# Even tokens first in each block, and mixer B's far keys kept by parity, in one softmax

## The chip, the cores and the metric

One of the eight cores of a Trainium2 chip runs the whole kernel. Its engines are TensorE (PE, with its weight loads, PEld), VectorE (DVE), ScalarE (ACT), GpSimd (POOL) and SyncE (SP); each works through its own instructions in order and waits for the others through semaphores. All DMAs here are issued by SP. The metric is the device time of one execution in microseconds (us); two kernels are compared by runs on the same chip.

## The reference

One decoder block on 1024 tokens with a model width of 1024, in float32:

- modulated RMS norm of x, and one projection to the queries, keys and values of two mixers
- mixer A: 8 query heads on 2 key/value heads, each query sees the last 128 keys, with a sink in the denominator
- mixer B: 8 heads of width 64, a mixture of three dilated windows:

```python
B_BRANCHES = ((128, 1), (512, 4), (2048, 16))
for window, d in B_BRANCHES:
    # query t attends keys t, t-d, ..., t-(window//d)*d
    o, lse = banded_attention(to_sub(q), to_sub(k), to_sub(v), window // d, return_lse=True)
w = softmax(stack(lses))            # branches weighted by their softmax denominators
ob = sum(w * stack(outs))
```

- RMS norm of both mixers' outputs, an output projection, a norm, a gate and the residual; then an MLP (1024 to 4096, squared ReLU, back) with norms, a gate and the residual.

Weighting the branches by their denominators is the same as one softmax over all causal keys in which a key counts as often as branches reach it: 0 to 3 times. A key more than 128 back is reached only by d = 4 and d = 16, so its distance is a multiple of 4.

## The kernel before, in words

The kernel is one program for one core. A planner (`Sched`) runs while the program is built: each step has an engine, a planned duration, events it depends on, buffers it takes (`Res`) and gives back, and a priority. The planner plays the clocks of the engines forward and emits each engine's instructions in the order that this gives. On the chip that order is fixed. PE has several streams (`dense`, `s`, `t`, `pv` and others), among which `prefer` chooses: projections go first while attention is less than 0.8 units behind them, attention otherwise.

The projection is cut into six units u: 0 and 1 are mixer A's, 2 to 5 mixer B's, two heads each. Attention on a unit runs while the next units are projected. Float32 precision comes from operands split into a high and a low part, each product being two or three matmuls.

Attention of mixer B goes by items (u, tp, h): one head h and one pair tp (0 to 3) of query blocks of 128 tokens. Most items come in the order of u and tp; the item (4, 3, 1) comes after (5, 0, 1). Each item takes these steps:

- `s_b`: for each of the two query blocks qb, the scores of all (qb+1) x 128 keys, in chunks of up to 512 columns of one PSUM bank (L1240, PE; two banks, `r_s`). On each chunk one DVE instruction adds a mask with the logarithm of how often a key counts, writes the row to `p_sb` and takes the running minimum of the negated scores into `mn` (L1259). ACT takes the exponential and its sum (L1266), DVE the reciprocal (L1269), POOL scales the row (L1271).
- `t_pv`: in tp+1 chunks, each of two key blocks, PE transposes the probabilities of both query blocks (L1345, L1348), ACT copies the high part and DVE makes the low part (`ph`, L1359 and L1363), and PE multiplies with v (L1375, L1378, L1380). The stationary operand holds v's high and low parts side by side, so the output has 128 rows; the moving operand is the high and then the low part of the probabilities, 256 columns each.
- at the end of an item ACT copies the 64 rows of v's low part out of PSUM (L1407), DVE adds the 64 others (L1411), and SP stores the head's output to DRAM (L1414).

A probability buffer (`p_sb`, NP = 4 of them) holds an item's two rows for tp below 2, one row otherwise. In `evac` the projected v is transposed to tokens by rows and split (`vs`, L936 and L939). After the last projection eight output blocks (`out_block`, L1606 to L1717) begin as soon as their heads are done, and then the MLP runs in products of half matrices (L2093 to L2095 and the sums around them). `finish` stores the result, 128 tokens by 512 columns at a time (L2211).

Of the kernel before, what the change touches and what calls it, by code (L numbers as in the profile page):

```python
# [10 lines left out]
F32 = mybir.dt.float32  # L11
# [47 lines left out]
CW_MA = CW_MB + 1024  # L59
# [36 lines left out]
def _host(inputs):  # L96
# [14 lines left out]
    h["positions"] = np.ascontiguousarray(inputs["positions"][0].reshape(TB, P).T)  # L111
# [5 lines left out]
def _constants(c):  # L117
    c[:, CW_ID:CW_ID + P] = np.eye(P, dtype=np.float32)
    p = np.arange(P)[:, None]
    d = p + 896 - np.arange(1024)[None, :]  # L120
    mult = ((d >= 0) & (d <= 128)).astype(int)
    mult += (d >= 0) & (d <= 512) & (d % 4 == 0)
    mult += (d >= 0) & (d % 16 == 0)
    neg = np.array([BIG, 0.0, -np.log(2.0), -np.log(3.0)], np.float32)
    c[:, CW_MB:CW_MB + 1024] = neg[mult]
    d = p + P - np.arange(256)[None, :]
    c[:, CW_MA:CW_MA + 256] = np.where((d >= 0) & (d <= 127), 0.0, BIG)
# [267 lines left out]
def hybrid_block(ctx: ExitStack, tc: tile.TileContext, x, positions, w_ada, b_ada, g_attn_post, w_in, w_out,  # L395
# [33 lines left out]
    WR, WS, NP, NV, NK, NQ, NT, NO = 6, 2, 4, 3, 2, 2, 2, 2  # L429
# [3 lines left out]
    r_vt = Res(1)  # L433
    r_v, r_k, r_q, r_p, r_ph, r_ot, r_tmp = Res(NV), Res(0), Res(0), Res(NP), Res(NT), Res(NO), Res(1)
# [38 lines left out]
    vring = pool("vring", NV, "right", stack=rightv)  # L473
    prp = pool("prp", 1, stack=left1)
# [352 lines left out]
    qs, ks, vs, e_q, e_k, n_in = {}, {}, {}, {}, {}, {}  # L827

    acc_at = [(pj, "pj", r_pj)] * 2 + [(po, "o", r_o)] + [(psp, "s", r_s)] * 2 + [(pt, "t", r_t)]

    def evac(u, x, c, get_ps, done, r_bank):
# [109 lines left out]
        op("DVE", t_dv(256 * nh), f_vl, [e], gives=[(r_x, 1)], prio=2, after=posted)  # L941
# [110 lines left out]
    def open_attention():  # L1052
# [14 lines left out]
        masks = mkp.tile([P, 1280], F32, name="masks")  # L1067
        e_mask = load(lambda: nc.sync.dma_start(masks[:], consts[:, CW_MB:CW_MB + 1280]), 655360, prio=-20)
        mask_b = masks[:, 0:1024]
        mask_a = masks[:, 1024:1280]  # L1070
# [124 lines left out]
    UB = 2 * (2 * (0.108 + 0.117 + 0.173 + 4 * 0.227 + 0.108 + 0.117 + 0.173 + 0.227) + 0.107 * 36 + 0.43 * 10)  # L1195
# [5 lines left out]
    def count(it):  # L1201
        return it[1] + 1 if it[0] > 1 else (2 if it[1] else 1)
# [13 lines left out]
    def s_b(i, it, rec):  # L1216
        u, tp, h = it
        shared = tp < 2
        rec.e_p = []
        rec.held = 1 if shared else 2  # L1220
        for qi in range(2):
            qb = 2 * tp + qi
            W = (qb + 1) * P
            last_mn = None
            b = {}
            for c0 in range(0, W, 512):
                m = c0 // 512
                cw = min(512, W - c0)
                end = c0 + cw == W

                def f_s(c0=c0, cw=cw, m=m, qi=qi, qb=qb, W=W, b=b):
                    if m == 0:
                        if qi == 0 or not shared:
                            rec.tile = pprob.tile([P, 4 * 257], F32, name="p_sb", tag="p")
                        off = 2 * tp * P + P if shared and qi else 0
                        rec.p.append(rec.tile[:, off:off + W])
                        b["mn"] = small.tile([P, 2], F32, name="mn", tag="mn")
                    s = b["s", m] = psp.tile([P, 512], F32, name="s_ps", tag="s")
                    for hl in range(2):
                        T.matmul(s[:, :cw], qs[u, qb // 4][:, 2 * h + hl, qb % 4 * P:qb % 4 * P + P],  # L1240
                                 ks[u][:, h, c0:c0 + cw], start=(hl == 0), stop=(hl == 1))
                d = 2 * t_mm(cw)
                deps = e_k[u, c0 // 512] + e_q[u, qb // 4]
# [11 lines left out]
                e = pe_op("s", d, f_s, deps, takes=[(r_s, 1), (r_p, slot)], gives=gives, after=after)  # L1255

                def f_max(c0=c0, cw=cw, m=m, qi=qi, W=W, b=b):
                    mn = b["mn"]
                    V.tensor_tensor_reduce(rec.p[qi][:, c0:c0 + cw], b["s", m][:, :cw],  # L1259
                                           mask_b[:, 1024 - W + c0:1024 - W + c0 + cw], 1.0,  # L1260
# [1020 lines left out]
```

## Time and profile before

| what | us |
|---|---|
| runs of the kernel before | 1117.45, 1117.54, 1118.25 |
| median | 1117.54 |
| span of the profiled execution, first to last instruction | 1114.9 |
| median less span | 2.6 |
| PE busy | 1100.5 |
| DVE busy | 818.7 |
| ACT busy | 630.2 |

The span is that of the one execution that was profiled; its time from outside isn't listed apart from the three runs, and the 2.6 us stand for what lies around the span. Times in the profile count from the first instruction. Projections run from about 20 to 372 us, mixer B's scores from 161 to 406, output blocks from 372 to 493, the MLP from 493 to 1106.

### The profile page before, as it was taken

How to read it: one execution, taken by the hardware profiler on the slowest of the kernel's cores; microseconds unless marked ns; L12 is line 12 of the kernel's file. 1: busy time of each engine (PE TensorE's matmuls, PEld its weight loads, DVE VectorE, ACT ScalarE, POOL GpSimd, SP SyncE). 2: the span in 40 equal slices, each digit the busy share in tenths (PEclk: the TensorE clock that was granted, in tenths of full speed). 3: DMA queues.
4: the chain of work that ended last, by engine and by line, in shares of the span. 5: the costliest groups of instructions: out<-in, count | busy, mean ns of one | idle time of the engine just before them, and what ended most of it. 6: DMA issues, size and time to landing. Idle time of an engine off the chain costs nothing.

```text
span 1114.9 us, 15568 instructions
## 1 busy us (share of the span) xinstructions
PE 1100.5 (99%) x5393; PEld 917.4 (82%) x5393; DVE 818.7 (73%) x1386; ACT 630.2 (57%) x1092; POOL 249.7 (22%) x318
## 2 busy tenths in 40 slices
PE   8999999999999999999999999999999999999996
PEld 7788888888888888888888888888888888888885
DVE  7877776666777666689798654798643996537998
ACT  8768776464656666577674335643154632347542
POOL 2158768666742231110000000000000000000003
PEclk9999999999999999999999999999999999999998
DMA  9766667464513734656751369521578013584104
GB/s 350 216 193 189 196 218 233 154 207 157 189 41 143 259 108 129 226 214 241 279 216 38 108 241 330 180 76 40 199 269 308 26 57 113 189 319 153 39 19 151
DMA packets 94110, 195.39 MB, mean 175 GB/s; under 512 B 9008, under 2 KB 31664, under 8 KB 94032
## 3 DMA queue, kind: packets, MB, share of 16 engines
q1 hardware_dynamic: 94032, 194.40, 50.4%
q8 instruction: 43, 0.70, 0.3%
q14 instruction: 35, 0.29, 0.1%
HBM read 141.80 MB, written 33.03 MB: 157 GB/s over the span
## 4 chain that ended last, share of the span: by engine, by line
PE 86%; DVE 8%; issue 2%; ACT 1%; DMA 1%; POOL 0%; SPq 0%; POOLq 0%; DVEq 0%; ACTq 0%
PE mlp_ps L2094 17%; PE mlp_ps L2095 17%; PE mlp_ps L2093 17%; PE pj L957 5%; PE pj L960 5%; PE pj L958 4%; PE s_ps L1240 3%; PE y_ps L1647 2%; PE y_ps L1649 2%; PE y_ps L1648 2%; PE o_ps L1375 2%; PE pt_ps L1345 1%; PE s_ps L1295 1%; PE o_ps L1387 1%; PE pt_ps L1352 1%
## 5 line engine op out<-in xcount | busy, mean ns | idle before, releaser
L2093 PE MATMUL mlp_ps<-hw 128*128 128x512 f32 x896 | 348.9, 389 | 0.1
L2094 PE MATMUL mlp_ps<-hw 128*128 128x512 f32 x896 | 348.6, 389 | 0.0
L2095 PE MATMUL mlp_ps<-hw 128*128 128x512 f32 x896 | 348.6, 389 | 0.0
L2093 PEld LDWEIGHTS mlp_ps<-hw 128*128 128x128 f32 x896 | 168.2, 188 | 35.8 <-DVE u L2130 0.6
L2094 PEld LDWEIGHTS mlp_ps<-hw 128*128 128x128 f32 x896 | 168.2, 188 | 35.0
L2095 PEld LDWEIGHTS mlp_ps<-hw 128*128 128x128 f32 x896 | 168.2, 188 | 34.6
L1857 DVE TENSOR_TENSOR hw<-w,hw 128x1024 fp32r<-128x1024 f32 x96 | 114.7, 1222 | 96.5 <-ACT hw L1850 96.3
L1850 ACT CAST hw<-w 128x1024 fp32r<-128x1024 f32 x96 | 97.7, 1048 | 126.9 <-PE mlp_ps L2095 86.2
L2203 POOL TENSOR_TENSOR st<-st,nhalf 128x1 f32<-128x1 f32 x8 | 8.0, 1010 | 591.8 <-DVE st L2201 591.8
L957 PE MATMUL pj<-hw,w_hl 128*128 128x512 f32 x240 | 102.3, 426 | 0.0
L960 PE MATMUL pj<-hw,w_hl 128*128 128x512 f32 x240 | 94.7, 394 | 0.0
L958 PE MATMUL pj<-hw,w_hl 128*128 128x512 f32 x240 | 94.3, 393 | 0.0
L1363 DVE TENSOR_TENSOR ph<-pt_ps,ph 128x512 fp32r<-128x512 f32 (+1 forms) x110 | 69.2, 647 | 30.9 <-ACT ph L1359 30.5
L1850 ACT CAST hw<-u 128x1024 fp32r<-128x1024 f32 x48 | 48.6, 1051 | 63.2 <-PE mlp_ps L2095 63.2
L1359 ACT CAST ph<-pt_ps 128x512 fp32r<-128x512 f32 (+1 forms) x110 | 58.3, 555 | 31.1 <-PE pt_ps L1348 25.2
L1857 DVE TENSOR_TENSOR hw<-u,hw 128x1024 fp32r<-128x1024 f32 x48 | 57.0, 1220 | 17.8 <-ACT hw L1850 17.8
L1266 ACT ACTIVATE p_sb<-p_sb,mn 128x128 f32<-128x128 f32 (+3 forms) x64 | 49.7, 777 | 33.5 <-DVE mn L1259 31.7
L1271 POOL TENSOR_SCALAR p_sb<-p_sb,den 128x128 f32<-128x128 f32 (+3 forms) x64 | 48.9, 769 | 73.8 <-DVE den L1269 67.1
L2151 DVE TENSOR_TENSOR yacc<-yacc,mlp_ps 128x512 f32<-128x512 f32 x96 | 62.1, 683 | 3.3 <-PE mlp_ps L2095 3.3
L1107 POOL TENSOR_TENSOR ada_acc<-ada_acc,wa_st 128x512 f32<-128x512 f32 x42 | 56.6, 1347 | 3.5
L960 PEld LDWEIGHTS pj<-hw,w_hl 128*128 128x128 f32 x240 | 45.1, 188 | 10.4
L1647 PE MATMUL y_ps<-hw,oh 128*128 128x512 f32 x128 | 52.0, 406 | 0.0
(215 smaller groups left out, 1971.9 us busy)
## 6 DMA issues: line engine op xcount, KB each, us to landing
hw<-s_dram SPq DMA_DIRECT2D x84, 512.0 KB, 4.3
wa_st<-in_w_ada SPq DMA_DIRECT2D x32, 512.0 KB, 4.9
w<-in_w_up SPq DMA_DIRECT2D x32, 512.0 KB, 5.7
w<-in_w_down SPq DMA_DIRECT2D x32, 512.0 KB, 7.1
s_dram<-hw SPq DMA_DIRECT2D x28, 512.0 KB, 3.9
qt<-hl SPq DMA_DIRECT2D x40, 256.0 KB, 2.9
w_st<-in_w_in SPq DMA_DIRECT2D x36, 256.0 KB, 3.0
x_sb<-in_x SPq DMA_DIRECT2D x16, 512.0 KB, 5.4
```

What stands on the lines that cost most here:

```text
L957: T.matmul(ps, w[:, 0, n], h[0], start=(k == 0), stop=False)
L958: T.matmul(ps, w[:, 1, n], h[0], start=False, stop=False)
L960: T.matmul(ps, w[:, 0, n], h[1], start=False, stop=(k == KC - 1))
L1359: A.copy(b["ph"][:, 0, :w], b["pt"][:, :w])
L1363: V.tensor_tensor(b["ph"][:, 1, :w], b["pt"][:, :w], b["ph"][:, 0, :w].bitcast(F32), ALU.subtract)
L1647: T.matmul(ps[:], b["oh"][:, k], wh[:, c0:c0 + 512], start=(k == 4 * m), stop=False)
L1850: A.copy(out[j][0], flat(src[j]))
L1857: V.tensor_tensor(out[j][1], flat(src[j]), out[j][0].bitcast(F32), ALU.subtract)
L2093: T.matmul(ps[m][:], sh, mh, start=starts and k == 0, stop=False, **kw)
L2094: T.matmul(ps[m][:], sh, ml_, start=False, stop=False, **kw)
L2095: T.matmul(ps[m][:], sl, mh, start=False, stop=k == 3, **kw)
L2151: e = op("DVE", t_dv(512), lambda: V.tensor_tensor(y(), y(), ps[m][:], ALU.add), [e, ml.e_y[tb, n]], gives=gives, prio=1)
```

## The change

- The host puts each block of 128 tokens in the order even ones, then odd ones: x and the positions are reordered before the launch, and each store of the result becomes two, one for each parity, that write every second row.
- Mixer B's masks are made for that order; there are two of 640 columns, one for each query block of a pair, in place of one of 1024.
- Scores are still computed for all keys. When DVE adds the mask, it keeps from key blocks below 2 tp (the far ones) only the 64 keys of the query's parity: an instruction for the even half of the partitions and one for the odd half. The last key blocks (the near ones, 256 columns for tp above 0) are kept whole. The row is then 128 tp + 256 wide instead of up to 1024, and one softmax runs over it.
- PV has a near chunk (the moving operand is the high and low parts at once, up to 512 columns) and far chunks, in which 128 rows hold the keys of one parity of two blocks. For these a copy of v (`vf`) is made by four DMAs per unit and half, which put the keys of one parity of two blocks under each other. The output in PSUM has the high and low parts' halves side by side, and one more DVE instruction per item adds them.
- Probability buffers go from 4 to 3, and tp = 2 shares one; the planner's numbers follow. The list `TILED` is empty, so the branches under it emit nothing.

The diff, cut to its core:

```diff
+    h["x"] = np.ascontiguousarray(h["x"].reshape(1, TB, 64, 2, D).transpose(0, 1, 3, 2, 4)).reshape(1, S, D)
...
-    WR, WS, NP, NV, NK, NQ, NT, NO = 6, 2, 4, 3, 2, 2, 2, 2
+    WR, WS, NP, NV, NK, NQ, NT, NO = 6, 2, 3, 3, 2, 2, 2, 2
+    NF = (1, 1)
+    TILED = ()
...
+        def f_vf():
+            t = vf[u, x] = vfar.tile([P, np_, 2, 2, 2, 64], F32R, name="v_far", tag=f"vf{x}", bufs=NF[x])
+            for k in range(2):
+                for y in range(2):
+                    nc.sync.dma_start(t[64 * y:64 * y + 64, :, k].bitcast(F32),
+                                      vs[u, x][64 * k:64 * k + 64, y:2 * np_:2].bitcast(F32))
+        e_vf[u, x] = load(f_vf, 262144 * np_, [e], takes=[(r_vf[x], 1)], prio=-11, n=4)
...
+    def s_runs(qb):
+        if qb < 4:
+            return [(0, qb + 1)]
+        return [(0, 4), (4, qb + 1)] if qb != 4 else [(0, 3), (3, 5)]
...
+    def pv_steps(tp):
+        n0 = P * tp
+        if not tp:
+            return [[(0, 0), (1, 0), (1, P)]]
+        steps = [[(0, n0), (0, n0 + P), (1, n0), (1, n0 + P)]]
+        for j in range(0, tp, 2):
+            steps.append([(qi, P * i) for i in range(j, min(j + 2, tp)) for qi in range(2)])
+        return steps
...
+                        if whole:
+                            src = src[:, from_:from_ + nb]
+                        else:
+                            src = src.rearrange("p (b c t) -> p b c t", c=2, t=64)[:, from_:from_ + nb // 64, c]
+                            p, msk = (t.rearrange("p (b t) -> p b t", t=64) for t in (p, msk))
+                        V.tensor_tensor_reduce(p, src, msk, 1.0, mn[:, n0 - 1:n0] if n0 else BIG, ALU.add, ALU.min,
+                                               mn[:, n0:n0 + 1])
...
+    def score_parts(tp, qi, qb, m, w):
+        whole = slice(0, P)
+        if not tp:
+            return [(whole, 0, 0, w)]
+        nf = 2 * tp
...
+        a, z = s_runs(qb)[m]
+        out = []
+        if a < nf:
+            for c in range(2):
+                out.append((slice(64 * c, 64 * c + 64), 64 * a, 0, 64 * (min(z, nf) - a)))
+        if z == qb + 1:
+            out.append((whole, 64 * nf, (qb - 1 - a) * P, 256))
+        return out
...
-                for s2 in range(2):
-                    T.matmul(o[:, :256], v0, ph[:, s2, 0:256], start=(ch == 0 and s2 == 0), stop=False)
...
+                if not ch:
+                    blocks = [(2 * tp, (0, 1) if not tp else (1, 2), slice(0, 256))]
+                    if tp:
+                        blocks.append((2 * tp - 1, (0,), slice(0, P)))
+                    blocks.append((2 * tp + 1, (len(steps[0]) - 1,), slice(P, 256)))
+                    for n, (j, at, to) in enumerate(blocks):
+                        T.matmul(o[:].rearrange("p (s q) -> p s q", s=2)[:, :, to],
+                                 vs[u, j // 4][:, j % 4, h].rearrange("p s d -> p (s d)"),
+                                 ph[:, :, at[0] * P:(at[-1] + 1) * P], start=n == 0,
+                                 stop=last and n == len(blocks) - 1, skip_group_check=True)
+                else:
+                    n = len(steps[ch]) // 2
+                    for k in range(n):
+                        j = 2 * (ch - 1) + k
+                        for c in range(2):
+                            T.matmul(o[:].rearrange("p (s q c t) -> p s q c t", s=2, q=2, c=2)[:, :, :, c],
+                                     vf[u, j // 2][:, j % 2, c, h].rearrange("p s d -> p (s d)"),
+                                     ph[:, :, 256 * k:256 * k + 256].rearrange("p s (q c t) -> p s q c t", q=2, c=2)[:, :, :, c],
+                                     start=False, stop=last and k == n - 1 and c == 1, skip_group_check=True)
...
+            if isb and it[1:] == (3, 1):
+                gives += [(r, 1) for r in r_vf]
...
+                V.tensor_tensor(ob["tmp"][:, :256], rec.o[0:64, 256:512], ob["tmp"][:, :256], ALU.add)
                 V.tensor_tensor(ob["ot"][:], rec.o[0:64, :256], ob["tmp"][:, :256], ALU.add)
...
+            def f_out(hf=hf):
+                dst = out[tb * P:(tb + 1) * P, 512 * hf:512 * hf + 512].rearrange("(t c) d -> c t d", c=2)
+                for c in range(2):
+                    nc.sync.dma_start(dst[c], s.x[64 * c:64 * c + 64, 512 * hf:512 * hf + 512])
```

More of the change, by code (lines that the diff above doesn't have):

```diff
@@ L58 @@
 CW_MB = HEAD
-CW_MA = CW_MB + 1024
+CW_MA = CW_MB + 1280
 CW = CW_MA + 256
@@ L1217, in s_b, with f_s @@
         u, tp, h = it
-        shared = tp < 2
+        shared = tp < 3
         rec.e_p = []
         rec.held = 1 if shared else 2
+        nf = 2 * tp
+        W = [P, 2 * P] if not tp else [P * tp + 2 * P] * 2
         for qi in range(2):
             qb = 2 * tp + qi
-            W = (qb + 1) * P
             last_mn = None
             b = {}
[L1226 to L1231, printed above, removed]
+            w = W[qi]
+            seen = [0, 0]
+            runs = n_runs(qb)
+            for m in range(runs):
+                end = m == runs - 1
+                def f_s(m=m, qi=qi, qb=qb, w=w, b=b, end=end):
                     if m == 0:
@@ L1335, in t_pv @@
         isb = it[0] > 1
-        w = 384 if isb and last else 512
+        steps = pv_steps(it[1]) if isb else None
+        w = P * len(steps[ch]) if isb else 512
         r_ob = r_x if i % 2 else r_o
@@ L1342, in f_t @@
             if isb:
[L1343 to L1348 removed]
+                for n, (qi, c0) in enumerate(steps[ch]):
+                    T.transpose(p[:, n * P:n * P + P], rec.p[qi][:, c0:c0 + P], ident)
             else:
```

146 lines of the change are left out of this document (93 added, 53 removed).

## The prediction

> **What bounds the kernel now.** I read the page first (span, busy times, chain), then a table of stages, then the PE timeline inside mixer B's attention, then DVE by shape.
>
> ```profile
> span 1114.9 us, 15568 instructions
> PE 1100.5 (99%) x5393; PEld 917.4 (82%) x5393; DVE 818.7 (73%) x1386; ACT 630.2 (57%) x1092; POOL 249.7 (22%) x318
> ```
> ```profile
> PE 86%; DVE 8%; issue 2%; ACT 1%; DMA 1%; POOL 0%; SPq 0%; POOLq 0%; DVEq 0%; ACTq 0%
> ```
>
> PE is the bound, by busy time and by the chain. A matmul's record is longer than the distance to the next one, so busy time can't price a matmul; below I use start-to-start distances.
>
> The columns of the stage table are the stretch, its length, then busy time (and instructions) of PE, weight loads, DVE, ACT, POOL, then granted clock and DMA share.
>
> ```profile
> core 0: us, PE busy (x) PEld busy (x) DVE busy (x) ACT busy (x) POOL busy (x), PEclk, DMA share, GB/s
> 60.00:160.00 100.00, 99.47 (x550) 83.30 (x549) 77.66 (x220) 76.57 (x214) 72.94 (x113) 1.00 0.66 207
> 160.00:390.00 230.00, 229.33 (x1332) 196.37 (x1331) 160.91 (x417) 136.37 (x287) 129.37 (x142) 1.00 0.50 172
> 502.00:530.00 28.00, 27.86 (x127) 22.59 (x126) 27.34 (x36) 20.63 (x34) 0.55 (x1) 1.00 0.66 243
> 557.00:585.00 28.00, 28.00 (x126) 23.17 (x124) 25.50 (x26) 20.75 (x31) 0.00 (x0) 1.00 0.60 221
> ```
>
> Mixer B's attention fills most of 160 to 390, woven with the last projections and the first output block. PE idles 0.7 us there, so every matmul taken out shortens the stretch one for one, as long as nothing else becomes the bound. DVE is the next engine, at 70% (160.91 of 230). The two MLP stretches are for later: DVE at 98% and at 91%, and PE idle 0.14 and 0.00 us.
>
> **PE: what goes.** Per unit of two heads the code runs every step for both heads; mixer B has 8 heads (4 units), and tp is the pair of query blocks, 0 to 3.
>
> Transposes: a chunk has 4, the last of a pair 3, with tp+1 chunks: 3+7+11+15 = 36 per head. After, the lists of steps hold 3, 6, 8 and 10: 27 per head. 72 fewer in all.
>
> PV: before, 32 matmuls of 256 columns and 8 of 128 per head. After, tp=0 has one of 512 and one of 256; each other pair has one of 512 and two of 256 on the near keys, plus two of 256 for each pair of far blocks (1, 2, 3 of them). That is 4 of 512 and 19 of 256 per head.
>
> Scores: all keys are still multiplied, so the columns stay; only block 4's split 512+128 turns into 384+256, which takes away two 128-column matmuls per head and makes their columns part of wider ones.
>
> ```profile
> 205.72 0.41 PE L1375 MATMUL o_ps<-ph,v_hl 128*128 128x256 f32 x2
> ...
> 206.69 0.38 PE L1345 MATMUL pt_ps<-head,p_sb 128*128 128x128 f32 x2
> 206.90 0.27 PE L1348 MATMUL pt_ps<-head,p_sb 128*128 128x128 f32 x1
> 207.01 0.38 PE L1345 MATMUL pt_ps<-head,p_sb 128*128 128x128 f32 x2
> 207.23 0.38 PE L1348 MATMUL pt_ps<-head,p_sb 128*128 128x128 f32 x2
> 207.37 0.47 PE L957 MATMUL pj<-hw,w_hl 128*128 128x512 f32 x1
> 207.68 0.39 PE L958 MATMUL pj<-hw,w_hl 128*128 128x512 f32 x1
> 207.91 0.40 PE L960 MATMUL pj<-hw,w_hl 128*128 128x512 f32 x1
> 208.15 0.62 PE L1240 MATMUL s_ps<-kt,qt 128*128 128x512 f32 x2
> ```
> ```profile
> 209.54 0.33 PE L1378 MATMUL o_ps<-ph,v_hl 128*128 128x128 f32 x2
> 209.71 0.45 PE L957 MATMUL pj<-hw,w_hl 128*128 128x512 f32 x1
> 210.00 0.39 PE L958 MATMUL pj<-hw,w_hl 128*128 128x512 f32 x1
> ```
>
> - 512 columns: 207.68 to 208.15 is two, 0.235 each.
> - 256 columns: 205.72 to 206.69 is two full chunks, 8 matmuls: 0.121 each.
> - transposes: 206.69 to 207.68 holds seven and one of 512: (0.99 - 0.235)/7 = 0.108. (The next matmul's start is late by what the last transpose seems to save, hence the longer stretch.)
> - 128 columns: 209.54 to 210.00 holds two and one of 512: 0.112 each, nearly the price of 256.
>
> Transposes: 72 x 0.108 = -7.8 us. PV: before 256 x 0.121 + 64 x 0.112 = 38.1, after 32 x 0.235 + 152 x 0.121 = 25.9, so -12.2. Scores: 16 x (0.112 - 0.06) = -0.8, 0.06 being half of the 256-column price. **PE in sum: -20.8 us.**
>
> The trace has no matmul whose moving operand is strided; the 96 far ones read and write runs of 64 elements. Bounds: the same 0.121, or twice that (+11.6 us). I take the first: 512 and 256 columns cost the same per column, and the weight load, 188 ns, hides under neighbours either way.
>
> [...]
>
> **DVE: what is added.**
>
> ```profile
> L1363 DVE TENSOR_TENSOR ph<-pt_ps,ph 128x512 fp32r<-128x512 f32 x78 | 52.7, 687 | 23.6 <-ACT ph L1359 23.2
> L1259 DVE CUSTOM_DVE_ANT_0 p_sb<-s_ps,masks 128x512 f32<-128x512 f32 x40 | 27.4, 684 | 5.3 <-PE s_ps L1240 4.7 <-POOL wa_st L1106 0.3 <-issue 0.2
> L1363 DVE TENSOR_TENSOR ph<-pt_ps,ph 128x384 fp32r<-128x384 f32 x32 | 17.5, 552 | 7.3 <-ACT ph L1359 7.3
> L1411 DVE TENSOR_TENSOR ot<-o_ps,otmp 64x256 f32<-64x256 f32 x32 | 13.2, 411 | 5.3 <-ACT otmp L1407 5.1
> L1259 DVE DVE_READ_ACCUMULATOR2_ANT mn<- 128x1 f32 x96 | 7.8, 81 | 0.0
> L854 DVE TENSOR_TENSOR hl<-pj,tab 64x512 f32<-64x512 f32 x10 | 6.8, 684 | 3.7 <-PE pj L960 1.7 <-POOL wa_st L1106 1.1 <-issue 0.5
> L1259 DVE CUSTOM_DVE_ANT_0 p_sb<-s_ps,masks,mn 128x512 f32<-128x512 f32 x8 | 5.9, 742 | 0.2
> L1259 DVE CUSTOM_DVE_ANT_0 p_sb<-s_ps,masks,mn 128x384 f32<-128x384 f32 x8 | 4.9, 611 | 0.6
> L1259 DVE CUSTOM_DVE_ANT_0 p_sb<-s_ps,masks 128x384 f32<-128x384 f32 x8 | 4.4, 550 | 0.5 <-PE s_ps L1240 0.5
> L1259 DVE CUSTOM_DVE_ANT_0 p_sb<-s_ps,masks,mn 128x256 f32<-128x256 f32 x8 | 3.9, 484 | 1.1 <-PE s_ps L1240 0.6
> L1259 DVE CUSTOM_DVE_ANT_0 p_sb<-s_ps,masks 128x256 f32<-128x256 f32 x8 | 3.3, 413 | 0.5 <-PE s_ps L1240 0.4
> L1259 DVE CUSTOM_DVE_ANT_0 p_sb<-s_ps,masks,mn 128x128 f32<-128x128 f32 x8 | 2.8, 347 | 2.3 <-PE s_ps L1240 1.8
> L1259 DVE CUSTOM_DVE_ANT_0 p_sb<-s_ps,masks 128x128 f32<-128x128 f32 x8 | 2.3, 284 | 1.2 <-PE s_ps L1240 1.2
> ```
>
> Mask-and-minimum (L1259): the far part of a score chunk is now taken in two instructions, one for each half of the partitions, and half the partitions cost as much as all (64x512: 684; 128x512: 687). Each instruction carries its 81 ns read of the accumulator. Line through the plain rows: 128 gives 284, 256 gives 413, so 192 gives 348 and 64 gives 218; a running minimum adds 63. With the read, per head in ns: block 0 365; 1 494; 2 and 3 each 2x365+565 = 1295; 4 2x429+2x362+565 = 2147; 5 2x494+565 = 1553; 6 and 7 each 2x494+2x428+565 = 2409. Sum 11.97 us from 26 instructions, times 8 = 95.7. Before, the group's rows sum to 62.7 for 96 instructions. **+33.0 us.**
>
> Low parts of the probabilities (L1363): mixer B has 48 chunks of 512 and 32 of 384 now (50.6 us), then 40 of 512, 8 of 384 and 16 of 256 at about 411 (38.5): **-12.1 us.** One more add of 64x256 per item (L1411): **+13.2 us.** DVE in sum +34.1, of which some nine tenths lie before 390: 160.91 + 31.7 = 192.6 us of work in a stretch that PE would run in 230 - 19.5 = 210.5: 91%. ACT's exponentials and copies and POOL's scaling run over 3456 instead of 4608 columns per head; both engines only lose work, at 59% and 56%, so that is worth nothing.
>
> What this DVE load costs PE the trace can't show directly. From below: 0, since the stretch at 98% left PE 0.14 us idle. From above: attention never runs DVE above the 77.7% of 60 to 160, and 192.6/0.777 = 248 us, which is 37 above 210.5. The nearest row by share is 557 to 585, 91% and no idle; but there a PE step doesn't pass through DVE twice as here (minimum, then low parts), and instructions come half as often. I take 4 us, an estimate of 2% of the stretch.
>
> **Queues, copies, tail.** Per unit and half, v is copied across partitions in 4 DMAs: 32 more on SP's queue, 3.1 MB, at a DMA share of 0.50.
>
> ```profile
> 176.89 1.20 SPq L900 DMA_DIRECT2D qt<-hl  x2
> ```
> ```profile
> qt<-hl SPq DMA_DIRECT2D x40, 256.0 KB, 2.9
> ```
> ```profile
> 369.43 0.34 PE L1378 MATMUL o_ps<-ph,v_hl 128*128 128x128 f32 x2
> ...
> 375.23 0.34 PE L1378 MATMUL o_ps<-ph,v_hl 128*128 128x128 f32 x2
> ```
> ```profile
> L2211 SPq DMA_DIRECT2D out_x<-x_sb x16: 332/332/337, 1089.5 to 1111.7; - x16
> ```
>
> At 0.6 us an issue, a copy takes 2.4 to issue and 2.9 to land: 5.3 us. Its buffer is single, so it waits for the last PV of the unit before, and behind it on SP stand mixer B's output stores and the next w_in tiles; the far PV of (unit, 1, 0) waits for it. The tightest place is unit 5: (4,3,1) ends at 369.43 and (5,1,0)'s last chunk ran at 375.23, 5.8 later. It fits by half a microsecond, and where it doesn't, projections and the first output block fill PE: 0, within the 4 us above. The last store is two issues instead of one: +0.33 at the end, uncovered. Masks grow from 640 to 768 KB long before their first use; three instead of four probability buffers hold as many items, as pair 2 now shares one; the reordering of x and positions is on the host: all 0, the first two covered by projections.
>
> **Sum.** -20.8 + 4 + 0.3 = -16.5. On the span that is 1098.4; the median of the runs, 1117.54, stands 2.6 above the span, so I forecast **1101**.
>
> **Rivals.**
> 1. *DVE becomes the bound (slower).* In the same in-order queue DVE evacuates scores (two banks), rotates projections and makes low parts; PE waits at each. It decides where DVE can't pass 192.6/230 = 84% during attention. At the 77.7% of 60 to 160 the stretch is 248 us: +18, 1136. At 88%, 219 us: 1107. For it: that 77.7% is the most seen with attention; against it: 98% and 91% with PE full. [...]
> 2. *The far matmuls run at half rate:* 1101 + 11.6 = 1113.
> 3. *The v copy is waited for:* three unit borders at 5.3 us with nothing to fill PE: 1101 + 16 = 1117, no change. Against it: 5.8 us and more between the two PVs, and projections at hand.
> 4. *No stall at all:* 1097.
>
> **How the numbers follow.** 2.2 us (0.2%) is about what can be told from no change: 1115.3 to 1119.7. Forecast with stalls of some microseconds, 1098 to 1108: 0.64. No stall or more saved, below 1098: 0.08. Rival 2, or rival 1 in part, 1108 to 1115: 0.12. Rival 3 or a larger part of rival 1 within 0.2%: 0.06. Rival 1, slower: 0.10. Faster 0.84, same 0.06, slower 0.10. The range leaves out slower, same and the ends: 1096 to 1114.
>
> **What would show it.** PE with 216 transposes and 184 PV matmuls in mixer B, those of 256 columns at 0.12 us start to start; 208 mask instructions, 95 us; DVE near 90% until attention ends; that end about 17 us earlier, and the MLP as long as before. I am wrong if PE shows idle time behind the mask or low-part instructions of more than 10 us, if far matmuls start 0.24 apart, or if PE waits for the copied v.

## The result, and the profile after

The changed kernel takes **1109.37 us** (median of 4 runs, 1109.05 to 1110.98) against 1117.49 us for the kernel before beside it: a ratio of 0.9931, 95% interval 0.9917 to 0.9945. It is 8.1 us faster where 16.5 were forecast. The profiled execution is the slowest of the four (1110.98 from outside, span 1109.2); the spans of the other three are 1107.3 to 1107.7.

The page's span, busy times and chain of the changed kernel:

```profile
span 1109.2 us, 15399 instructions
PE 1086.1 (98%) x5185; PEld 894.8 (81%) x5185; DVE 840.3 (76%) x1616; ACT 614.2 (55%) x1080; POOL 246.8 (22%) x324
```
```profile
PE 71%; DVE 13%; DMA 6%; issue 4%; ACT 2%; POOL 2%; SPq 1%; POOLq 0%; DVEq 0%; ACTq 0%
```

PE's share of the chain fell from 86% to 71%; DVE's rose from 8% to 13%. PE still bounds the kernel, but it waits more often. The stage tables show where. The first is the kernel before, cut at its last projection (372), its last PV of mixer B (420) and its last output block (493); the second is the changed kernel, cut at the same events (362, 424, 486).

```profile
160.00:372.00 212.00, 211.66 (x1226) 181.45 (x1224) 146.92 (x377) 123.88 (x262) 125.22 (x137) 1.00 0.47 161
372.00:420.00 48.00, 47.67 (x280) 40.84 (x279) 35.51 (x86) 32.93 (x58) 12.73 (x13) 1.00 0.53 178
420.00:493.00 73.00, 72.45 (x354) 60.08 (x354) 49.63 (x92) 47.23 (x74) 11.63 (x17) 1.00 0.53 183
```
```profile
160.00:362.00 202.00, 199.26 (x1068) 164.46 (x1068) 165.22 (x570) 112.22 (x255) 120.67 (x138) 1.00 0.57 185
362.00:424.00 62.00, 58.33 (x294) 46.14 (x294) 48.94 (x148) 38.02 (x68) 14.08 (x19) 1.00 0.52 167
424.00:486.00 62.00, 60.37 (x296) 49.53 (x295) 40.74 (x73) 42.15 (x71) 9.60 (x13) 1.00 0.57 200
```

The projections end 10 us earlier, the attention 3 us later. The stage between them grew from 48 to 62 us, and PE idles 3.7 us of it instead of 0.3. DVE went from 69% (146.92 of 212) to 82% (165.22 of 202) in the first stage.

Busy time hides short waits, since a matmul's record is longer than the distance to the next (0.39 us against 0.227 in the MLP of the kernel before). So I priced each matmul near the shortest distances between like neighbours in these traces (0.227, 0.171 and 0.114 us for 512, 384 and 256 columns, 0.1085 for 128 and fewer), summed these per stage and took the sum from the stage's length. What is left is time lost to PE:

| stage | lost before | lost after |
|---|---|---|
| start to 160 | 12.4 | 13.1 |
| 160 to the last projection | 7.4 | 12.3 |
| to the last PV of mixer B | 2.5 | 8.4 |
| to the MLP | 1.4 | 2.8 |
| MLP | 0.1 | 0.0 |
| after the last matmul starts | 8.6 | 10.2 |
| sum | 32.4 | 46.8 |
| matmuls at these prices | 1082.4 | 1062.3 |

PE has 20.1 us less to do, and 14.4 us more are lost: 12.2 between 160 and the MLP, 1.6 at the end, 0.7 before 160. The two profiles are not of median runs: 1.8 us lie around the span (1110.98 against 1109.2), not the 2.6 of the table before the prediction, so the kernel before was profiled at about 1116.7, 0.8 under its median, and the changed one 1.6 above its own. Between the medians, what is lost ahead of the tail is the remainder 20.1 - 1.6 - 8.1 = 10.4 us.

What PE waited for from 155 to 500 (line, what it waited for, us in total, times, longest), first in the kernel before, then in the changed one:

```profile
PE pm_o L1619 <- DVE o_sb L1613: 0.4, 1, 0.4
PE o_ps L1375 <- DVE ph L1363: 0.3, 1, 0.3
PE s_ps L1240 <- DVE mn L1259: 0.3, 1, 0.3
```
```profile
PE pm_o L1738 <- DVE o_sb L1732: 1.5, 2, 1.1
PE o_ps L1481 <- DVE ph L1466: 1.4, 2, 0.9
PE s_ps L1311 <- DVE mn L1345: 1.0, 4, 0.4
PE s_ps L1311 <- DVE y_sb L1787: 0.7, 1, 0.7
PE y_ps L1766 <- DVE mn L1345: 0.7, 1, 0.7
PE o_ps L1490 <- DVE ph L1466: 0.6, 1, 0.6
```

All that are shown are DVE's, 5.9 us in the changed kernel: low parts (`ph`), masks (`mn`), and steps of the output blocks on the same engine. (Of the three rows of the changed kernel that are left out, 1.0 us, 0.2 is ACT's.) One of them in PE's timeline:

```profile
200.38 0.40 PE L981 MATMUL pj<-hw,w_hl 128*128 128x512 f32 x1
201.28 0.73 PE L1481 MATMUL o_ps<-ph,v_hl 128*128 128x512 f32 x3 [0.51 <-DVE ph L1466]
```

A projection can't step in there: the order on PE is fixed, and PV is next.

### The profile page after: what moved, and what is told of

It is laid out like the page before. It is cut to its first block, busy times and chain, and to the rows that moved or that the text cites. A ratio compares the mean times of both kernels' runs of the same rounds, so it can differ in the third digit from the quotient of the medians.

```text
span 1109.2 us, 15399 instructions
## 1 busy us (share of the span) xinstructions
PE 1086.1 (98%) x5185; PEld 894.8 (81%) x5185; DVE 840.3 (76%) x1616; ACT 614.2 (55%) x1080; POOL 246.8 (22%) x324
## 4 chain that ended last, share of the span: by engine, by line
PE 71%; DVE 13%; DMA 6%; issue 4%; ACT 2%; POOL 2%; SPq 1%; POOLq 0%; DVEq 0%; ACTq 0%
PE mlp_ps L2212 17%; PE mlp_ps L2214 17%; PE mlp_ps L2213 17%; PE pj L978 3%; PE pj L981 3%; PE pj L979 3%; DVE p_sb L1345 2%; DMA wa<-in_w_ada 2%; PE s_ps L1311 2%; DMA o_sb<-o_dram 2%; DMA w_st<-in_w_in 1%; PE s_ps L1401 1%; PE y_ps L1766 1%; PE y_ps L1768 1%; PE y_ps L1767 1%
## 5 line engine op out<-in xcount | busy, mean ns | idle before, releaser
L978 PE MATMUL pj<-hw,w_hl 128*128 128x512 f32 x240 | 99.3, 414 | 0.0
L981 PE MATMUL pj<-hw,w_hl 128*128 128x512 f32 x240 | 94.6, 394 | 0.0
L979 PE MATMUL pj<-hw,w_hl 128*128 128x512 f32 x240 | 94.3, 393 | 0.0
L1466 DVE TENSOR_TENSOR ph<-pt_ps,ph 128x512 fp32r<-128x512 f32 (+2 forms) x94 | 57.4, 628 | 22.2 <-ACT ph L1462 21.8
L1462 ACT CAST ph<-pt_ps 128x512 fp32r<-128x512 f32 (+2 forms) x94 | 49.1, 541 | 29.7 <-PE pt_ps L1451 25.7
L1353 ACT ACTIVATE p_sb<-p_sb,mn 128x640 f32<-128x640 f32 (+3 forms) x64 | 42.0, 657 | 33.5 <-DVE mn L1345 30.8
L1358 POOL TENSOR_SCALAR p_sb<-p_sb,den 128x640 f32<-128x640 f32 (+3 forms) x64 | 39.8, 626 | 74.2 <-DVE den L1356 57.3
L981 PEld LDWEIGHTS pj<-hw,w_hl 128*128 128x128 f32 x240 | 45.1, 188 | 10.2
```

The lines of the kernel that those rows point to most:

```text
L978: T.matmul(ps, w[:, 0, n], h[0], start=(k == 0), stop=False)
L979: T.matmul(ps, w[:, 1, n], h[0], start=False, stop=False)
L981: T.matmul(ps, w[:, 0, n], h[1], start=False, stop=(k == KC - 1))
L1466: V.tensor_tensor(b["ph"][:, 1, :w], b["pt"][:, :w], b["ph"][:, 0, :w].bitcast(F32), ALU.subtract)
```

## The experiments

Theory A: DVE's added work delays attention's steps, and PE waits for them in a fixed order. Rivals: the loss is a bad draw of the order; it comes from the copies of v; it sits at the end of the kernel.

"In the same order" means that only the body of a step was edited: every other instruction stands where it stood on its engine. Otherwise the planner made a new order.

### DVE's added work, taken away and put in, in the same order

**Without the second halves of the masks** (leaves out the choice of parity for odd queries):

```diff
-                        mn = b["mn"][rows]
+                        rows = rows if whole else slice(0, P); mn = b["mn"][rows]
...
-                        V.tensor_tensor_reduce(p, src, msk, 1.0, ...
+                        if whole or c == 0: V.tensor_tensor_reduce(p, src, msk, 1.0, ...
```

> The changed kernel with one mask instruction over all 128 partitions in the place of the first half's, and none in the place of the second's, in an otherwise unchanged order (unlike the earlier run of this edit, where the order moved too); it leaves out the choice of parity for the odd queries. VectorE loses 72 mask instructions with their read-outs, about 72 x 0.50 = 36 us. Theory A: the time falls from 1109.4 to 1099 to 1103 us, the lower end if the copies of v are not waited for, the upper one if the 3.5 us of the earlier run return. Rival B: 1106 to 1109 us.

Measured: **1101.80** (1101.22 to 1103.58), ratio 0.9860 (0.9845 to 0.9874). The mask groups by line, of the changed kernel and of this one (busy us, mean ns):

```profile
L1345 DVE CUSTOM_DVE_ANT_0 p_sb<-s_ps,masks 64x256 f32<-64x256 f32 (+3 forms) x112 | 40.0, 362 | 4.1 <-PE s_ps L1311 2.5
L1345 DVE CUSTOM_DVE_ANT_0 p_sb<-s_ps,masks,mn 128x256 f32<-128x256 f32 (+2 forms) x96 | 38.5, 401 | 3.8 <-PE s_ps L1311 1.5
L1345 DVE DVE_READ_ACCUMULATOR2_ANT mn<- 64x1 f32 (+1 forms) x208 | 16.4, 79 | 0.0
```
```profile
L1345 DVE CUSTOM_DVE_ANT_0 p_sb<-s_ps,masks,mn 128x256 f32<-128x256 f32 (+2 forms) x72 | 30.5, 424 | 8.0 <-PE s_ps L1311 7.3
L1345 DVE CUSTOM_DVE_ANT_0 p_sb<-s_ps,masks 128x128 f32<-128x128 f32 (+2 forms) x64 | 22.5, 357 | 4.5 <-PE s_ps L1311 4.2
L1345 DVE DVE_READ_ACCUMULATOR2_ANT mn<- 128x1 f32 x136 | 11.0, 81 | 0.0
```

The records shrink from 94.9 to 64.0 us, DVE's busy time in the page by 26.8 (840.3 to 813.5), the time by 7.6. With the same order and the same copies, the second halves cost 7.6 us. DVE now waits longer for scores (4.1 + 3.8 becomes 8.0 + 4.5).

**Without the extra add of the low parts** (leaves out the product of the low parts of the probabilities; one line of `f_o2`), alone and together with the edit above:

```diff
-                V.tensor_tensor(ob["tmp"][:, :256], rec.o[0:64, 256:512], ob["tmp"][:, :256], ALU.add)
```

> The changed kernel without the extra add of the low parts (line 1530's predecessor, 32 instructions of 0.413 us), in the same order; it leaves out the product of the low parts of the probabilities. VectorE loses 13.2 us. If a microsecond of VectorE's work costs what it cost in the run without the second halves (7.6 us for 32.3 us, 0.24), the time falls by 3.1 us to 1106.3 (1105 to 1107.5). If only the mask instructions, which lie between scores and exponential, cost anything: 1109 to 1110.

> Both of VectorE's additions taken away in the same order: one mask instruction over 128 partitions for two halves, and no add of the low parts; it leaves out the choice of parity for the odd queries and the product of the low parts of the probabilities. VectorE has less to do than in the kernel before. If the price goes on evenly: 1101.8 - 3.1 = 1098.7. If VectorE has slack by then: 1100.5 to 1102. Either would leave the changed kernel's order about 15 to 19 us ahead of the kernel before, against the 20.1 us that TensorE saves less 1.5 us at the end.

Measured: **1105.18** (1104.64 to 1108.77), ratio 0.9902 (0.9883 to 0.9921); together **1102.41** (1101.95 to 1102.98), ratio 0.9869 (0.9854 to 0.9884). The add alone costs 4.2 us (its four runs spread over 4.1, so this price is known to some 2 us), the masks alone 7.6, both 7.0. The prices don't add: with the masks gone, the add costs nothing that can be told; with the add gone, the masks still cost some 2.8. The pages' DVE busy time falls by 11.0, 26.8 and 37.8 us in the three runs, so a microsecond of it is worth 0.38, 0.28 and 0.19 us: there is no fixed price for an instruction, and it falls as DVE gets slack.

**The kernel before with each mask instruction cut in two**, result kept, first unknown to the planner (same order), then planned with its durations:

```diff
-                    mn = b["mn"]
-                    V.tensor_tensor_reduce(rec.p[qi][:, c0:c0 + cw], b["s", m][:, :cw], ...
+                    for a, z, n, mn in ((0, cw // 2, 2 * m, b["mn"]), (cw // 2, cw, 2 * m + 1, b["mn"])):
+                        V.tensor_tensor_reduce(rec.p[qi][:, c0 + a:c0 + z], b["s", m][:, a:z], ...
```

> The kernel before with each mask instruction of mixer B cut into two instructions over half of the keys, in the same place of the same order: 192 for 96, TensorE's work and order as in the kernel before. From the rows of the two traces an extra instruction costs about 0.14 us of fixed time, 0.063 us for the operand that carries the running minimum and 0.08 us for its read-out, so VectorE gets about 96 x 0.28 = 27 us more, as much as the change gave it. Theory A (VectorE's load delays the attention and TensorE waits behind it): the kernel before loses what the changed one lost, 1125 to 1131 us. Rival B (the loss is the changed order, not the load): within 3 us of 1117.5. A price in between shares it out.

> The kernel before with each mask instruction cut in two, as in before_split (1128.4), but planned with the two instructions' durations. If the price of 27 us more on VectorE is set by its load: 1125 to 1130 again. If it was dear only since the plan did not know of it: 1120 to 1124, which is the 0.24 us per microsecond of the changed kernel (1117.4 + 6.4 = 1123.8) or less.

Measured: **1128.43** (1127.33 to 1129.32), ratio 1.0095 (1.0080 to 1.0110); planned, **1123.44** (1121.33 to 1124.64), ratio 1.0052 (1.0037 to 1.0067). Stage 160 to 390 of the two:

```profile
160.00:390.00 230.00, 225.35 (x1279) 188.52 (x1277) 170.98 (x565) 130.42 (x274) 126.34 (x139) 1.00 0.46 160
```
```profile
160.00:390.00 230.00, 225.65 (x1284) 191.44 (x1283) 172.65 (x565) 130.01 (x273) 127.98 (x139) 0.99 0.47 161
```

PE's work is that of the kernel before, and still PE idles 4.4 to 4.7 us where it idled 0.7. DVE's busy time rose by 18.7 and 19.1 us, at a price of 11.0 and 5.7. With a plan that knows the load, that is 0.30 us for each microsecond, about the 0.28 (7.6 / 26.8) of the second halves. Theory A holds in both kernels. In this one pair the order that doesn't know of the load costs twice as much; a new order of the same work alone moved the kernel before by 1.4 us (below).

**Without the copies of v**, same order (the far keys' values are other ones):

```diff
-                for y in range(2):
+                for y in range(0):
                     nc.sync.dma_start(t[64 * y:64 * y + 64, :, k].bitcast(F32),
...
-                                      vf[u, j // 2][:, j % 2, c, h].rearrange("p s d -> p (s d)"),
+                                      vs[u, tp // 3][:, (2 * j + c) % 4, h].rearrange("p s d -> p (s d)"),
```

> The changed kernel without the 32 copies of v, in the same order on every engine (the earlier run of this edit had another order); the far products read v as it was stored, so the far keys' values are other ones. If the copies are hidden: within 1 us of 1109.4. If their issues on SP, their traffic or a wait for them cost anything: 1106 to 1108.4.

Measured: **1108.98** (1107.92 to 1109.44), ratio 0.9924 (0.9908 to 0.9941). 0.4 us lies within the spread: the copies are hidden.

### The same work in other orders

**The first run without the second halves** let the planner know, which changed the order:

```diff
-            for c in range(2):
-                out.append((slice(64 * c, 64 * c + 64), 64 * a, 0, 64 * (min(z, nf) - a)))
+            out.append((whole, 64 * a, -1, 64 * (min(z, nf) - a)))
```

> Leaves out the choice of the odd queries' keys: the far part of a chunk is masked by one DVE instruction over all 128 partitions, which takes the even keys for every query. 136 mask instructions instead of 208, by the rows some 31 us less DVE work in durations; PE, copies, buffers and stores as in the changed kernel. Theory (PE waits for the mask instructions' extra DVE time): the lost PE time in 160 to 420 us falls back to about that of the kernel before, 10 us, and the time to about 1100 us. Rival (buffers or copies): PE's lost time stays near 20 us and the time within 2 us of 1109.4. Rival (planned durations too short): about half of it comes back, 1105.

Measured: **1106.99** (1106.12 to 1107.91), ratio 0.9910 (0.9892 to 0.9928). It gave back 2.4 us where the same edit in the same order gives 7.6. In its order PE waited 3.5 us for a copied v at the border of units 4 and 5; elsewhere it doesn't. Right behind that wait its granted clock is halved for 3.4 us, from 368.6 to 372.0 (over the span it is 0.996, with the same edit in the same order 0.997); 3.5 and half of 3.4, an estimate, are about the 5.2 us that are missing. It was expected at about 1100; by itself this run would have spoken for the wrong theory.

**A longer and two shorter planned mask durations** (the two shorter ones with the store edit of the next section), **a smaller lead of the projections, and no copies in a new order**:

```diff
-                    last_mn = op("DVE", t_dv(nb) + 0.06, f_max, ...
+                    last_mn = op("DVE", t_dv(nb) + 0.11 + 0.1 * (n0 > 0), f_max, ...   (plan_cost)
+                    last_mn = op("DVE", t_dv(nb), f_max, ...                           (plan_low)
+                    last_mn = op("DVE", t_dv(nb) + 0.03, f_max, ...                    (plan_low2)
...
-        if st.d < 5.99 and st.d - st.a < (LEAD if st.d < 4.5 else 0.5):
+        if st.d < 5.99 and st.d - st.a < 0.5:                                          (lead_half)
...
-        if not isb:
+        if True:
             return                                                                     (no_copy)
```

> Same instructions, but the planner counts 0.05 us more for a mask instruction and 0.1 more again where it goes on from a running minimum, near the start-to-start distances in the trace. Theory (DVE time itself): within 2 us of 1109.4, since the work is the same. Rival (the order was planned with too short DVE steps, so that PE's next step stands too early in its queue): 4 us or more faster, 1105 or below.

> The changed kernel (with the odd half of the last block's stores on ScalarE's queue) planned with 0.06 us less for each mask instruction: same work, other order. If the order given was only one draw among those within 5 us: 1104 to 1114. If a planner that believes in a lighter VectorE sends the attention out too early and TensorE waits in line: 1111 to 1115; if it keeps the projections as cover for longer: 1104 to 1107.

> As plan_low, with 0.03 us less: a second draw of the order. 1104 to 1114; together with plan_low, the longer plan (+6.8) and the lead of 0.5 (+1.4) it gives the spread that orders of the same work have here.

> The changed kernel in which the projections are preferred up to a lead of 0.5 over the attention all the way, where it was 0.8 for the first three quarters: the same work, other order, the projections held back. If the loss comes from projections that run out ahead of the attention: 1102 to 1107 us, with a later end of the projections than 362 us. If the order is only noise around a price that the load sets: 1108 to 1114 us, either side.

> Leaves out the copies of v by parity (32 DMAs) and the waits for them; the far matmuls read other rows of v, same shapes. Theory (DVE time): the copies are hidden, within 1.5 us of 1109.4. Rival (copies hold up SP's queue or the far PV): 4 us or more faster.

The same was done to the kernel before (mask durations planned 0.05 longer, 0.1 more with a running minimum):

> The kernel before with the same instructions, planned with 0.05 us more for each mask instruction and 0.1 us more where it carries a running minimum, as was done to the changed kernel (there +6.8 us). If the price of another order depends on VectorE's slack (70% busy here, 82% there): within 2 us of 1117.5. If any other order costs as much, whatever the load: 1121 to 1126 us.

Measured, with the time from the last projection to the first product of an output block:

| kernel | us (lowest to highest) | ratio to before, 95% | projection to output block |
|---|---|---|---|
| changed, order as given | 1109.37 (1109.05 to 1110.98) | 0.9917 to 0.9945 | 3.6 |
| lead_half | 1110.75 (1110.06 to 1112.80) | 0.9919 to 0.9952 | 9.3 |
| no_copy | 1113.86 (1113.12 to 1114.31) | 0.9955 to 0.9980 | 10.0 |
| plan_cost | 1116.14 (1115.38 to 1117.82) | 0.9979 to 0.9998 | 20.0 |
| plan_low | 1116.63 (1115.24 to 1118.24) | 0.9982 to 1.0001 | 16.5 |
| plan_low2 | 1122.78 (1120.61 to 1123.32) | 1.0029 to 1.0059 | 8.5 |
| before_plan | 1118.77 (1117.82 to 1120.25) | 1.0002 to 1.0021 | 0.3 |

The last column comes from rows like these (last projection product, first output product; the final pair of times is first and last start), of the kernel before, the changed one and plan_low:

```profile
L960 PE MATMUL pj<-hw,w_hl x240: 387/395/402, 67.6 to 372.2; 128*128 128x512 f32 x120
L1647 PE MATMUL y_ps<-hw,oh x128: 387/389/500, 372.5 to 492.6; 128*128 128x512 f32 x128
```
```profile
L981 PE MATMUL pj<-hw,w_hl x240: 387/394/402, 67.9 to 362.4; 128*128 128x512 f32 x120
L1766 PE MATMUL y_ps<-hw,oh x128: 387/390/499, 366.0 to 485.4; 128*128 128x512 f32 x128
```
```profile
L981 PE MATMUL pj<-hw,w_hl x240: 387/393/402, 68.8 to 364.7; 128*128 128x512 f32 x120
L1766 PE MATMUL y_ps<-hw,oh x128: 387/389/774, 381.2 to 493.3; 128*128 128x512 f32 x128
```

None of the five other orders is cheaper than the one given, which speaks against a bad draw as the reason of the loss; `lead_half`, 1.4 us slower, can't be told apart from it. The others cost 4.5 to 13.4 us here, the one before 1.4 (1118.77 against 1117.41 beside it). `no_copy`, `plan_cost`, `plan_low` and `plan_low2` came out above everything that was expected of them. `lead_half` was to end the projections later than 362 us, but they end at 360.8, so it doesn't tell whether their early end is to blame. The slow orders share a stretch in which the projections have run out and the first output block isn't ready, so attention alone feeds PE. The column doesn't rank them, though: plan_low2 has the shortest such stretch of the five and is the slowest; I summed 20.8 us lost between 160 and its last projection, against 12.3 as given.

Beside the waits there is a second price. Four-microsecond stretches of plan_low (length, PE, weight loads, DVE, ACT, POOL, granted clock, DMA share, GB/s), then two of the changed kernel at its own emptiest place:

```profile
366.00:370.00 4.00, 3.03 (x21) 2.47 (x20) 3.13 (x12) 1.70 (x4) 0.00 (x0) 1.00 0.88 337
370.00:374.00 4.00, 2.24 (x10) 1.07 (x8) 3.77 (x20) 1.85 (x6) 1.15 (x2) 0.96 1.03 236
374.00:378.00 4.00, 2.79 (x11) 2.52 (x12) 2.77 (x14) 2.98 (x6) 0.72 (x2) 0.50 0.41 111
378.00:382.00 4.00, 4.00 (x15) 3.61 (x16) 3.79 (x12) 2.15 (x4) 0.67 (x1) 0.50 0.65 243
382.00:386.00 4.00, 4.00 (x16) 3.28 (x16) 2.76 (x10) 1.62 (x5) 0.69 (x1) 0.76 0.93 285
```
```profile
362.00:366.00 4.00, 2.81 (x16) 1.78 (x15) 2.80 (x12) 2.96 (x7) 0.58 (x1) 1.00 1.06 366
366.00:370.00 4.00, 3.27 (x14) 2.15 (x15) 3.89 (x12) 2.25 (x5) 0.59 (x1) 1.00 1.01 260
```

Four microseconds at 56% busy (2.24 of 4), and the granted clock falls to 0.50 and stays there for some 10 us (0.3, 4, 4 and 1.9 by the rows), also when PE is full again (378 to 382). The changed kernel dips to 70% and keeps 1.00. No single wait of PE in plan_low is over 1.21 us from 155 to 500. The busy share of a stretch doesn't settle it alone, though: plan_low2 keeps its clock after four microseconds at 34%:

```profile
343.00:347.00 4.00, 1.36 (x10) 0.88 (x8) 2.33 (x5) 2.87 (x4) 0.00 (x0) 1.00 0.06 26
347.00:351.00 4.00, 3.48 (x18) 2.75 (x19) 3.63 (x14) 2.71 (x9) 2.45 (x4) 1.00 0.00 0
```

All five other orders of the changed kernel have such a halving between 350 and 410 us: 3.4 us long in lead_half (0.66 from 390 to 395) and no_copy (0.91 from 362 to 380), 6.8 in plan_cost (0.86, 0.50 and 0.96 in the five-microsecond stretches from 355) and plan_low2 (0.72 and 0.60 from 395), 10.2 in plan_low. The changed kernel has none there. Within the one of plan_low, matmuls of 512 columns start 0.42 to 0.43 us apart (381.80, 382.23, 382.65); behind it, 0.23 to 0.24 (384.15 to 384.86). So by these distances a halving costs at most about half of its length (an estimate), and it is a part of the price of these orders and not the whole. What sets it off, no run here shows.

### The end, and two attempts at a better version

**One store for two** (rows leave in even-odd order), **and the second of the last two pairs on ScalarE's queue** (result kept):

```diff
-                for c in range(2):
-                    nc.sync.dma_start(dst[c], s.x[64 * c:64 * c + 64, 512 * hf:512 * hf + 512])
+                nc.sync.dma_start(out[tb * P:(tb + 1) * P, 512 * hf:512 * hf + 512], s.x[:, 512 * hf:512 * hf + 512])   (one_store)
...
+                    (nc.scalar if c and tb == TB - 1 else nc.sync).dma_start(dst[c], s.x[64 ...                         (tail_act)
```

> Each store of the result is one DMA of 128 partitions as before (rows then lie in the even-odd order). The stages up to the MLP stay. Reading of the two traces: the last DVE end to the last landing is 4.76 us instead of 3.2, so 1.5 us faster than 1109.4, 1107.9. As predicted (one issue more at 0.33): 0.3 us faster.

> The changed kernel with the odd half of the last token block's two stores issued on ScalarE's queue instead of SP's: two of the last four issues of 0.57 us leave the chain at the end. If the end is the row of issues on SP: 1108.2 to 1108.5 (-0.9 to -1.2 us). If the 2.3 us of a strided transfer's landing set it: within 0.4 us of 1109.4.

Measured: **1107.88** (1107.38 to 1108.74), ratio 0.9916 (0.9900 to 0.9932), and **1109.09** (1108.34 to 1109.65), ratio 0.9928 (0.9913 to 0.9943). The stores of the changed kernel:

```profile
L2333 SPq DMA_DIRECT2D out_x<-x_sb x32: 466/571/597, 1082.2 to 1105.7; - x32
```

A store of every second row took SP 571 ns to issue, where a whole one took 332; the last two stores, two issues before and four now, stand at the end of the chain. From the last matmul's start to the end of the span it takes 10.4 us in the changed kernel, 8.9 with one store, 9.6 with two of four on the other queue. That is 1.5 and 0.8 less; the medians moved by 1.5 and 0.3, and the second can't be told from none.

**The low parts' add on GpSimd** (this kernel has no store edit, whatever its label says), **and mixer B's reciprocals on GpSimd** as a power multiplied by twice, with the store edit:

```diff
+                A.copy(ob["tmp"][:, 256:], rec.o[0:64, 256:])
-                V.tensor_tensor(ob["tmp"][:, :256], rec.o[0:64, 256:512], ob["tmp"][:, :256], ALU.add)
+            e = op("POOL", t_ptt(256), lambda: G.tensor_tensor(ob["tmp"][:, :256], ob["tmp"][:, :256], ob["tmp"][:, 256:], ALU.add), [e], prio=0)
...
-            e = op("DVE", 0.08, lambda b=b: V.reciprocal(b["den"][:], b["den"][:]), [e], prio=0)
+            e = op("POOL", 0.6, lambda b=b: G.tensor_tensor(b["den"][:], b["den"][:], nhalf[:, :1], ALU.pow), [e], prio=0)
```

> The changed kernel with the add of the low parts on GpSimd: ScalarE copies both low parts out of PSUM (0.37 us more for each item), GpSimd adds them, VectorE makes the last add alone; same result. VectorE loses 13.2 us, the order is planned anew. If VectorE's load is the price: 1105 to 1107, and the order may take or give up to 5 us as it did in the runs before; if the longer way to the item's end (a hop to GpSimd of about 0.8 us) holds PSUM banks up: 1110 to 1114.

> The changed kernel, same result, with mixer B's 64 reciprocals (0.156 us each, 10.0 us of VectorE) put on GpSimd as a power of -1/2 that the following scale multiplies by twice, and with the odd half of the last block's stores on ScalarE's queue. If VectorE's load in the projections is the price, at 0.24 to 0.32 us for each microsecond: 1106.0 to 1106.7 from 1109.1, give or take the order. If the added step of about 0.6 us on GpSimd, in line ahead of the transposes, costs more than that: 1110 or above.

Measured: **1112.59** (1110.97 to 1113.35), ratio 0.9958 (0.9943 to 0.9973), and **1126.08** (1125.47 to 1126.79), ratio 1.0076 (1.0059 to 1.0092). The second doesn't scale the rows as meant, for a reason that I didn't pursue; only its time is read. Both took work off DVE and lost: new orders, with 9.9 and 14.8 us between the last projection and the output blocks. In the second, one projection alone waits 4.7 us for a DMA (`hw<-wo_dram`), and GpSimd's steps themselves are long:

```profile
L1358 POOL TENSOR_SCALAR p_sb<-p_sb,den 128x128 f32<-128x128 f32 (+3 forms) x64 | 47.2, 744 | 2.1
L1356 POOL TENSOR_TENSOR den<-den,nhalf 128x1 f32<-128x1 f32 x64 | 37.6, 592 | 46.2 <-ACT p_sb L1353 41.2 <-DVE ph L1466 3.0 <-PE s_ps L1311 1.5
```

592 ns take the place of DVE's 156, between each row's exponential and its transposes. How much of the 17 us is this step and how much the order, no run tells apart. No version here beats the changed kernel with its whole work done by more than can be measured.

## Why the prediction was wrong

- **PE, -20.8: right.** At the neighbours' distances 72 transposes are 7.8, PV 36.1 - 24.6 = 11.5 and scores 0.8, 20.1 in all (20.4 at 0.118, the more usual distance at 256 columns). Far matmuls with strided operands cost no more than the contiguous ones of the prediction's row, 0.121 us for 256 columns. Four of them in PE's timeline:

```profile
207.59 0.64 PE L1490 MATMUL o_ps<-ph,v_far 128*128 128x256 f32 x4
208.06 0.40 PE L978 MATMUL pj<-hw,w_hl 128*128 128x512 f32 x1
```

  From 207.59 to 208.06 is 0.118 each. Rival 2 is out.
- **DVE, +34.1: right in records, not in time.** Masks 94.9 against 62.0, low parts 57.4 against 69.2, the add 13.2: +34.3. But busy time rose by only 21.6. Some 4 us are other DVE records that fell (all records together rose by 29.9, from 892.6 to 922.5); the rest is that a DVE record overlaps the next one:

```profile
211.38 0.42 DVE L1345 CUSTOM_DVE_ANT_0 p_sb<-s_ps,masks 64x256 f32<-64x256 f32 x1
211.73 0.07 DVE L1345 DVE_READ_ACCUMULATOR2_ANT mn<- 64x1 f32 x1
211.82 0.43 DVE L1345 CUSTOM_DVE_ANT_0 p_sb<-s_ps,masks 64x256 f32<-64x256 f32 x1
```

  0.49 us of records, 0.44 from one to the next. For PE I used distances; for DVE I summed records. So DVE stands at 82%, not 91%.
- **The stall, 4 us: the step that failed.** It is 10.4 in the median, at a lower DVE share than forecast. I chose a value near the lower bound because the MLP stretches run DVE at 91 to 98% without idle PE. There, no chain passes through DVE twice, as I wrote, and yet I let that row set the value. The loss table shows what I should have read from the kernel before: PE already lost 9.9 us between 160 and the last PV at DVE's 69 to 74%, of which the busy times show 0.7 as idle. For the same reason the sign that I named, over 10 us of idle time behind mask and low-part instructions, didn't show: the rows above have 3.7 (1.4 + 1.0 + 0.7 + 0.6). The runs put 7.6 on the second halves and 7.0 on all of DVE's additions together. The other 3 or so no run accounts for, but the table, made for the run without both additions, shows where they are: up to the last projection PE loses 6.5 us there, less than the 7.4 of the kernel before, and from there to the last PV 5.6 against 2.5. Why is open; the rest of the new order (three probability buffers, wider near chunks, projections that end earlier) wasn't tried apart.
- **Rival 1, DVE becomes the bound: its mechanism, not its form.** It had DVE saturate at 78 to 88%. Over the stage DVE isn't saturated: it is at 82% and still waits for scores. It is full in short stretches only (4.95 of 5 us from 340 to 345, with PE at 4.61). PE waits because the next step in a fixed order isn't ready, and that costs 0.2 to 0.4 us for each microsecond put on DVE, and 0.6 (11.0 for 18.7) in the one run whose order didn't know of it.
- **Copies of v, 0: right,** with one reservation: 0.4 us in this order, 3.5 us of waits at the border I had named in another.
- **Tail, +0.33: too small.** It measured 1.5: two issues of 332 ns became four of 571, 1.6 us more; I had added one issue at the old price.
- **"Attention ends about 17 us earlier": wrong,** it ends 3.4 later; the MLP starts 7.2 earlier (493.3 to 486.1) and is as long as before.

In sum, -20.1 + 10.4 + 1.6 = -8.1, where the forecast had -20.8 + 4 + 0.3. (The 10.4 is the remainder, so this sum can't fail to close; what stands on its own are the 7.0 to 7.6 of the runs.)

## What to carry to other kernels

In a fixed order an engine below saturation can still cost: with DVE at 82% of the stage, its additions cost 7.0 to 7.6 us here. Before the change, compare the sum of distances with wall time in the stage: where the bound engine already loses time that busy shares don't show, work added to the second engine isn't free, though what it costs had to be measured here (0.2 to 0.4 us for each microsecond). Test such a price by editing bodies in an unchanged order, in both kernels; a run that lets the planner move answers another question, and here it moved the time by up to 13 us. When work leaves the bound engine, look at what the saved work was covering: the projections ran out 10 us earlier, and most of what the runs on DVE leave open is lost behind them. That they had been the filler for the attention's waits is an argument; no run shows it.

## What was not expected of the hardware

- The granted clock halved for some 10 us after 4 us at 56% PE busy, with no single wait over 1.21 us (plan_low), and stayed at 1.00 after 4 us at 34% in plan_low2. In the five other orders the halvings lasted 3.4 to 10.2 us. Over the whole span the clock is 0.993 in plan_low, 0.989 with the power on GpSimd, 0.997 in the changed kernel and the one before.
- A store to every second DRAM row took its queue 571 ns to issue, for 64 partitions; one to consecutive rows from 128 partitions, twice the bytes, took 332 (in the kernel before).
- A matmul whose operand and output are runs of 64 elements went at 0.118 us for 256 columns; contiguous ones went at 0.121 in the row of the prediction.
